# GLA's state products half way between its other steps, fewer stored split operands, own slots for raw tiles

## The chip, the cores and the metric

The kernel runs on one core of a Trainium2 chip. The metric is the time of one execution in device microseconds; the kernel before takes 1884.07 us (median of three runs, 1876.56 to 1886.29).

## The reference, cut to what matters

One inference step of a hybrid decoder layer on 2048 prompt tokens and 8 x 8 sample tokens, all in float32. Two branches run side by side on the same input, are gated and added, projected and normalised:

```python
z = jnp.einsum('btd,dn->btn', x, w_in)                       # all input projections
o_att = swa_prompt(q, k, v, attn_sink, rel_table)            # window of 128, 8 heads, 2 KV heads
def step(S, xs):                                             # GLA, per head, chunk after chunk
    qt, kt = qc * jnp.exp(b), kc * jnp.exp(-b)
    kend = kc * jnp.exp(b_last[:, None] - b)
    A = jnp.where(causal, jnp.einsum('bthk,bshk->bhts', qt, kt), 0.0)
    o = jnp.einsum('bthk,bhkv->bthv', qt, S) + jnp.einsum('bhts,bshv->bthv', A, vc)
    S = jnp.exp(b_last)[..., None] * S + jnp.einsum('bshk,bshv->bhkv', kend, vc)
    return S, o
o_gla = o_gla * lax.rsqrt(jnp.mean(jnp.square(o_gla), -1, keepdims=True) + EPS) * gla_norm_w
h_att = jnp.einsum('bta,ad->btd', o_att * jax.nn.silu(g_att), w_pa)
h_gla = jnp.einsum('btv,vd->btd', o_gla * jax.nn.silu(g_gla), w_pg)
merged = jax.nn.sigmoid(r_att) * h_att + jax.nn.sigmoid(r_gla) * h_gla
y = layer_norm(DN_ALPHA * x + merged @ w_o, ln_g, ln_b)
```

The outputs are y for prompt and samples, the last K and V rows, and the GLA states of the prompt and of the eight samples.

## The kernel before, in words

**Passes.** The large projections are eight passes over the 2112 tokens, in this order: AT (attention's q, k, v and gate, 5 blocks of 256 columns), G0, G1, G2 (the GLA heads' k, q, v and gate, 4 blocks each), PA (attention's output, half the depth), RA and RG (the two merge gates), PG (GLA's output). Then the last projection with the layer norm. A pass multiplies in seven products of block sums (a Strassen-Winograd scheme; the products are numbered 1 to 7 and taken in a listed order, for G0 to G2 1, 2, 6, 7, 5, 3, 4). Tokens are taken in three sections `s`, so a *unit* is (pass, product, section), 21 to a pass. A unit runs over the pass's 4 or 5 blocks; each is a *group*: one PSUM tile `pd` of 128 x 352, filled by twelve matmuls.

**Splits.** Each float32 operand is split into a high and a low part (`xh`, `xl` for tokens, `wh`, `wl` for weights): ACT casts the high part (L148), DVE subtracts to get the low one (L149), both in two halves of 128 x 704 for a token tile. A group's twelve matmuls are four times `xh wh`, `xl wh`, `xh wl` (L1192, L1193, L1194). A raw token tile `xs` is loaded by `raw_x` two or three units ahead; `prep_x` splits it one unit ahead. Raw tiles and split tiles share a ring of seven slots, `xb`. The same token operands serve AT, G0, G1 and G2, so some splits are stored to DRAM (`sp..h`, `sp..l`) and loaded as they are by later passes: AT stores those of products 5 and 3, G0 those of 1, 2, 4, 6 and 7. So G0 splits five of seven products and loads two, and G1 and G2 load all.

**Work between the groups.** TensorE's order is written out by hand. After each group a *tick* passes, and functions filed under that tick by `at(t, ...)` issue their instructions behind the group. Attention (`att_...`, from pass AT's end to the middle of G1) and GLA (`gla_...`, from there to the end of RG) are filed this way; their PSUM tiles are a ring of four, `pa`. The order of the other engines (ACT, DVE, POOL, SP) comes from a scheduler, and each executes its list in order.

**GLA's step.** A head's 2048 tokens are taken in 16 steps of 128, some 4.4 ticks apart. In a step `gla_v` transposes v and the decayed keys (L955, L956) and ACT copies them to `gv` (L957); `gla_a` makes the intra-chunk matrix (L965), which DVE masks (L967); `gla_b` multiplies the query with the old state (L987), makes the state product (L989) and the intra-chunk output (L990), updates the state on DVE (L995) and normalises: square on ACT (L974), two tiny operations on POOL (L975, L976), scaling on ACT (L977) into `ring`; `gla_c` transposes the normalised output (L1003) and DVE multiplies it by the gate, `sg` (L1005). `gla_v` and `gla_a` of step i stand at tick u + i (in steps), `gla_c` at u + i + 3, so one step's `gla_v` and `gla_a` share a tick with the `gla_c` of three steps before. Each step takes five tiles of the ring of four.

**Samples.** After a head's last step `samp_a` and two calls of `samp_b` make the sample outputs (`ops`) and the new sample states (L1046, L1052), four sample columns in each call's half.

The pools on the left side of SBUF are exchanged as the program goes on: `c0` at the start, `ca` for attention, `cg` for GLA, `cm` at the end (`mpool`).

## Time and profile before

| | |
|---|---|
| median of three runs | 1884.07 us (1876.56 to 1886.29) |
| the profiled execution | 1890.45 us, its span 1888.7 us |
| mean granted TensorE clock | 0.977 |
| passes AT, G0, G1, G2 | 250.6, 255.3, 211.6, 221.0 us |
| passes PA, RA, RG, PG | 114.7, 225.5, 223.5, 182.2 us |
| last projection | 199.6 us |
| DMA | 496.20 MB, 263 GB/s in the mean |

Busy times are of the profiled execution. PE is TensorE's matmul, PEld its weight load, DVE the vector engine, ACT the scalar engine, POOL GpSimd, SP the engine that issues DMAs. In a row of waits stands who waited, at which line, for whom, the total in us, how often, and the longest. In a row of the timeline stand start, duration, engine, line, operation, tiles, and in brackets the idle time ahead of it and what ended it.

### The profile page before, as it was taken

The page shows a single profiled execution, that of the slowest core. Times are in us where ns is not written, and L with a number is a line of the kernel's source. Part 1 is how long each engine was busy: PE and PEld are TensorE (multiplying, and loading weights), DVE is VectorE, ACT ScalarE, POOL GpSimd, SP SyncE. Part 2 cuts the span into 40 slices and gives each one's busy share as a digit, 9 for nine tenths or more (in the row PEclk, how much of TensorE's full clock was granted, in tenths as well). Part 3 has the DMA queues.
Part 4 walks back from the last instruction along what each step waited for, and adds up shares of the span by engine and source line. Part 5 has one row for each costly group of instructions (what it writes and reads, how often), then busy time and mean ns, then how long its engine had stood idle before and what let it go on. Part 6 is the DMA issues. An engine that isn't in the chain of part 4 may idle for free.

```text
span 1888.7 us, 30578 instructions
## 1 busy us (share of the span) xinstructions
PE 1776.7 (94%) x10587; PEld 1632.9 (86%) x10587; DVE 1302.7 (69%) x2613; ACT 857.7 (45%) x1886; POOL 413.1 (22%) x554
## 2 busy tenths in 40 slices
PE   7999898999999999999998998999899999999998
PEld 6899887887888999989888888998899999987886
DVE  5738746868757665567668876887688566876666
ACT  4333334545553346466574765676656432211100
POOL 2230103200102001321133232124331233441111
PEclk9999998999999999999999999999999999999999
DMA  9857998978868799888876886798887887896431
GB/s 307 302 199 243 326 322 322 336 262 299 300 208 288 268 325 343 286 300 269 291 220 209 277 272 221 238 300 262 287 263 251 262 287 266 254 308 206 156 120 53
DMA packets 291835, 496.20 MB, mean 263 GB/s; under 512 B 29229, under 2 KB 216869, under 8 KB 291664
## 3 DMA queue, kind: packets, MB, share of 16 engines
q1 hardware_dynamic: 290752, 493.40, 77.9%
q8 instruction: 83, 1.36, 0.3%
q0 software_dynamic: 832, 0.72, 0.2%
q14 instruction: 72, 0.59, 0.1%
q10 hardware_dynamic: 96, 0.13, 0.0%
HBM read 338.06 MB, written 156.97 MB: 262 GB/s over the span
## 4 chain that ended last, share of the span: by engine, by line
PE 59%; DMA 13%; DVE 11%; ACT 6%; POOL 5%; issue 4%; SPq 1%; DVEq 0%; POOLq 0%; ACTq 0%
PE pd L1192 14%; PE pd L1193 13%; PE pd L1194 13%; PE pd L1239 3%; PE pd L1238 3%; PE pd L1237 3%; DMA ws<-w_g 2%; POOL ws L183 2%; DVE xl L149 2%; DMA x<-xT 2%; DMA ws<-w_ra 1%; PE pa L658 1%; PE pa L708 1%; PE pa L692 1%; DVE wl L149 1%
## 5 line engine op out<-in xcount | busy, mean ns | idle before, releaser
L1192 PE MATMUL pd<-xh,wh 128*128 128x352 f32 x2484 | 845.7, 340 | 36.3 <-ACT xh L148 19.0
L1193 PE MATMUL pd<-xl,wh 128*128 128x352 f32 x2484 | 811.3, 327 | 12.5 <-DVE xl L149 12.2
L1194 PE MATMUL pd<-xh,wl 128*128 128x352 f32 x2484 | 809.4, 326 | 0.0
L1192 PEld LDWEIGHTS pd<-xh,wh 128*128 128x128 f32 x2484 | 476.9, 192 | 77.5 <-ACT xh L148 30.7
L1193 PEld LDWEIGHTS pd<-xl,wh 128*128 128x128 f32 x2484 | 478.5, 193 | 20.0 <-DVE xl L149 17.9
L1194 PEld LDWEIGHTS pd<-xh,wl 128*128 128x128 f32 x2484 | 476.1, 192 | 0.0
L183 POOL TENSOR_TENSOR ws<-ws 128x256 f32<-128x256 f32 (+1 forms) x256 | 207.5, 836 | 702.6 <-DMA ws<-w_g 278.1
L149 DVE TENSOR_TENSOR xl<-xs,xh 128x704 fp32r<-128x704 f32 (+1 forms) x228 | 196.6, 892 | 53.5 <-ACT xh L148 49.9
L149 DVE TENSOR_TENSOR wl<-ws,wh 128x512 fp32r<-128x512 f32 (+1 forms) x231 | 158.5, 692 | 97.6 <-ACT wh L148 91.6
L148 ACT CAST wh<-ws 128x512 fp32r<-128x512 f32 (+1 forms) x231 | 134.1, 591 | 191.3 <-POOL ws L183 104.7
L148 ACT CAST xh<-xs 128x704 fp32r<-128x704 f32 (+1 forms) x228 | 155.6, 723 | 79.3 <-PE pd L1193 58.5
L975 POOL TENSOR_SCALAR sq<-sq 128x1 f32<-128x1 f32 (+1 forms) x68 | 25.9, 381 | 424.1 <-ACT ring L974 423.9
L1238 PE MATMUL pd<-woh,x 128*128 128x512 f32 x256 | 102.0, 398 | 0.9 <-DVE x L149 0.9
L1237 PE MATMUL pd<-woh,x 128*128 128x512 f32 x256 | 101.3, 396 | 0.4 <-ACT woh L148 0.2
L1239 PE MATMUL pd<-wol,x 128*128 128x512 f32 x256 | 101.2, 395 | 0.6 <-DVE wol L149 0.6
L148 ACT CAST x<-xst 128x384 fp32r<-128x384 f32 (+2 forms) x48 | 22.3, 486 | 137.1 <-PE pd L1238 107.9
L672 ACT ACTIVATE s<-s,nm 128x256 f32<-128x256 f32 (+1 forms) x128 | 62.4, 489 | 42.7 <-DVE nm L669 42.7
L977 ACT ACTIVATE ring<-pa,sq 128x256 f32<-128x256 f32 (+1 forms) x68 | 32.2, 473 | 94.6 <-POOL sq L976 94.6
L259 ACT COPY a<-pd 128x352 f32<-128x352 f32 x99 | 43.7, 451 | 53.5 <-PE pd L1194 53.1
L262 DVE TENSOR_TENSOR fin<-a,pd 128x352 f32<-128x352 f32 x99 | 50.3, 513 | 23.3 <-PE pd L1194 20.9
L287 DVE TENSOR_TENSOR a<-a,pd 128x352 f32<-128x352 f32 x93 | 47.5, 514 | 23.9 <-PE pd L1194 23.5
L283 DVE TENSOR_TENSOR fin<-a,pd 128x352 f32<-128x352 f32 x93 | 47.8, 514 | 22.1 <-PE pd L1194 21.4
(250 smaller groups left out, 2548.4 us busy)
## 6 DMA issues: line engine op xcount, KB each, us to landing
xs<-xc_d SPq DMA_DIRECT2D x45, 704.0 KB
ws<-w_g SPq DMA_DIRECT2D x108, 256.0 KB
xs<-xT SPq DMA_DIRECT2D x27, 704.0 KB
xc<-tt_d SPq DMA_DIRECT2D x48, 352.0 KB
ws<-w_at SPq DMA_DIRECT2D x45, 256.0 KB
ws<-w_ra SPq DMA_DIRECT2D x36, 256.0 KB
ws<-w_rg SPq DMA_DIRECT2D x36, 256.0 KB
ws<-w_pg SPq DMA_DIRECT2D x36, 256.0 KB
```

Source lines behind the costliest of these rows:

```text
L148: pin["a"] = nc.scalar.copy(dst_h, src)
L149: i = eng.tensor_tensor(dst_l, src, dst_h.bitcast(F32), ALU.subtract)
L183: nc.gpsimd.tensor_tensor(o[:, c], x[:, c], y[:, c], op)
L262: add(z, acc[p, s, 12], ps, ALU.add)
L283: add(z, u, ps, ALU.add)
L672: nc.scalar.activation(sl, sl, AF.Exp, bias=nm[:, h:h + 1], accum_out=sm[:, h:h + 1])
L1192: mm(ps, wh[:, ks], xh[:, ts], start=(k == 0), stop=False)
L1193: mm(ps, wh[:, ks], xl[:, ts], start=False, stop=False)
L1194: mm(ps, wl[:, ks], xh[:, ts], start=False, stop=(k == q.kh - 1))
L1237: mm(ps, xh[:, xs], hi, start=(k == 0), stop=False)
L1238: mm(ps, xl[:, xs], hi, start=False, stop=False)
L1239: mm(ps, xh[:, xs], lo, start=False, stop=(k == KT - 1))
```

## The change

Four edits:

- `gla_b` of step i is filed 3/2 steps after `gla_v` of step i, not 5/4. The two calls of `samp_b` are filed one tick later.
- The sample outputs are normalised inside the first `samp_b`, ahead of its state products, not after the second.
- AT stores no splits; G0 stores those of products 1, 2, 6, 7 and 4 as before. So G0, G1 and G2 load the raw tiles of products 5 and 3 and split them themselves.
- While the pool `ca` is open, raw tiles have two slots of their own in it (`xs`); `xb` then holds only split tiles.

```diff
     def mpool(name):
         mid.close()
+        M["name"] = name
         M["p"] = mid.enter_context(tc.tile_pool(name=name, bufs=1, side="left", reuse_waits="tile"))
...
-            x = mtile("xb", F32, "xs")[:, :n]
+            if M["name"] == "ca":
+                x = mt("xs", 4 * T, 2)[:, :n]
+            else:
+                x = mtile("xb", F32, "xs")[:, :n]
...
         def stores(self, i):
-            return i in ((5, 3) if self is passes[P_AT] else (1, 2, 4, 6, 7) if self is passes[P_G0] else ())
+            return self is passes[P_G0] and i in (1, 2, 6, 7, 4)
...
                     mm(B["ops"][32 * q:32 * q + 32, :HV], B["qz"][:, 4 * q + b, :], B["S0", 4 * q][:, b, :],
                        start=False, stop=(b == 3), tile_position=(0, 32 * q))
+            gla_norm(B, "s", B["ops"][:NS, :HV], NS)
         sp = [pa(), pa()]
...
-        if j0:
-            gla_norm(B, "s", B["ops"][:NS, :HV], NS)
...
-                at(tt(u + i + 5 / 4), lambda B=B, i=i: gla_b(B, i))
+                at(tt(u + i + 3 / 2), lambda B=B, i=i: gla_b(B, i))
...
-                at(o + 5, lambda B=B: samp_b(B, 0))
-                at(o + 7, lambda B=B: samp_b(B, 2))
+                at(o + 6, lambda B=B: samp_b(B, 0))
+                at(o + 8, lambda B=B: samp_b(B, 2))
```

In the changed program the lines are numbered a little higher (L1195 for L1192, L149 for L148, L993 for L989). Three places of the order follow; numbers behind a name tell buffers apart.

TensorE at one GLA step in pass G2, from `gla_c` to `gla_b`'s third product, before:

```order
L1003 MATMUL pa_8302<-ident_197,ring_7201 128x128 x2
L955 MATMUL pa_8306<-ident_197,zvv_8010 128x128 x2
L956 MATMUL pa_8306<-ident_197,ek_8086 128x128
L965 MATMUL pa_8311<-dm_8084,em_8085 128x128
L1192 MATMUL pd_8333<-xh_7907,wh_8018 128x352
...
L987 MATMUL pa_8350<-ring_7201,gb_7836 128x256
L989 MATMUL pa_8352<-gv_7203 128x256
L990 MATMUL pa_8350<-gv_7203,aper2_211 128x256
```

and now:

```order
L1007 MATMUL pa_8326<-ident_197,ring_7209 128x128 x2
L959 MATMUL pa_8330<-ident_197,zvv_8034 128x128 x2
L960 MATMUL pa_8330<-ident_197,ek_8099 128x128
L969 MATMUL pa_8335<-dm_8097,em_8098 128x128
L1195 MATMUL pd_8357<-xh_7931,wh_8042 128x352
...
L1195 MATMUL pd_8374<-xh_7931,wh_8169 128x352
...
L991 MATMUL pa_8394<-ring_7209,gb_7849 128x256
L993 MATMUL pa_8396<-gv_7211 128x256
L994 MATMUL pa_8394<-gv_7211,aper2_211 128x256
```

`gla_b` stood one group (a `pd` tile's twelve matmuls) behind the other three, and now stands two behind; the others keep their places.

ACT in pass G0, units (1,0) and (1,1); `xh_2806` and, in the changed program, `xh_2782` are the high part for unit (1,1), whose first group is `pd_2907` and now `pd_2883`. Before:

```order
L259 COPY a12_2857<-pd_2844 128x352
L259 COPY a12_2872<-pd_2859 128x352
L259 COPY a12_2887<-pd_2874 128x352
L148 CAST xh_2806<-xs_2598 128x704 x2
L259 COPY a12_2920<-pd_2907 128x352
L148 CAST wh_2903<-ws_2804 128x512
```

and now:

```order
L149 CAST xh_2782<-xs_2578 128x704 x2
L149 CAST wh_2796<-ws_2677 128x512
L149 CAST wh_2879<-ws_2780 128x512
L149 CAST wh_2967<-ws_2867 128x512
L311 ACTIVATE th_2752<-a12_834 128x352
L149 CAST xh_2869<-xs_2673 128x704 x2
L311 ACTIVATE th_2774<-a5_859 128x352
L263 COPY a12_2813<-pd_2800 128x352
L263 COPY a12_2833<-pd_2820 128x352
L263 COPY a12_2848<-pd_2835 128x352
L263 COPY a12_2863<-pd_2850 128x352
L263 COPY a12_2896<-pd_2883 128x352
```

The cast stood behind the copies of the four groups of unit (1,0); now it and the one for unit (1,2), `xh_2869`, stand ahead of all of them.

DVE in pass G2 at the end of unit (3,1), where the operand of unit (3,2) was loaded split before; `pd_9962` is the last group of (3,1), `pd_10007` the first of (3,2), `xl_9872` the low part that (3,2) needs. Now:

```order
L291 TENSOR_TENSOR a12_8121<-a12_8121,pd_9943 128x352
L291 TENSOR_TENSOR a12_8147<-a12_8147,pd_9962 128x352
L1009 TENSOR_TENSOR sg_9715<-pa_9981,sg_9715 128x2x64
L150 TENSOR_TENSOR xl_9872<-xs_9580,xh_9871 128x704 x2
L997 COPY ring_7209<-pa_9986 128x256
L314 SCALAR_TENSOR_TENSOR a12_8147<-th_9976,a12_8147 128x352
L291 TENSOR_TENSOR a12_8186<-a12_8186,pd_10007 128x352
```

The subtract stands behind the eviction of the unit before, with no group between that and its use.

## The prediction

> **What bounds the kernel now.** I read the page first, then the busy time by pass, then the waits of TensorE in the passes that the change touches, then single waits in the timeline.

> ```profile
> span 1888.7 us, 30578 instructions
> PE 1776.7 (94%) x10587; PEld 1632.9 (86%) x10587; DVE 1302.7 (69%) x2613; ACT 857.7 (45%) x1886; POOL 413.1 (22%) x554
> ```

> TensorE is busy for 94% of the span, so an edit off TensorE can win only what TensorE now waits: 1888.7 - 1776.7 = 112 us, and the time that it runs below full clock. By pass (us, then busy time of PE, PEld, DVE, ACT, POOL with counts, granted clock, DMA share, GB/s; the rows are G0, G2, RA and RG):

> ```profile
> 255.30:510.60 255.30, 234.46 (x1417) 207.17 (x1417) 180.23 (x337) 122.12 (x329) 35.65 (x44) 0.95 0.86 304
> 722.20:943.20 221.00, 210.97 (x1296) 201.60 (x1295) 137.46 (x335) 128.41 (x275) 48.58 (x84) 0.98 0.86 291
> 1057.90:1283.40 225.50, 214.65 (x1315) 202.60 (x1314) 180.67 (x398) 146.35 (x299) 59.68 (x83) 0.98 0.81 260
> 1283.40:1506.90 223.50, 210.31 (x1264) 198.73 (x1263) 160.07 (x329) 128.52 (x265) 72.05 (x96) 0.97 0.81 264
> ```

> G0 idles 255.3 - 234.5 = 20.8 us and loses 0.05 x 255.3 = 12.8 us to the clock. G2, RA and RG idle 10.0 + 10.9 + 13.2 = 34.1 us and lose 0.02 x 221 + 0.02 x 225.5 + 0.03 x 223.5 = 15.6 us. The waits of TensorE (total, times, longest), first in G0, then from 722 to 1507 us:

> ```profile
> PE pd L1192 <- ACT xh L148: 8.5, 6, 3.3
> PE pd L1193 <- DVE xl L149: 6.9, 8, 1.9
> ...
> PE pa L989 <- DVE sg L1005: 16.1, 10, 4.3
> PE pa L989 <- ACT gv L957: 7.0, 3, 2.6
> PE pa L1046 <- ACT ring L977: 4.2, 2, 3.6
> PE pa L989 <- ACT ak L957: 3.2, 3, 2.2
> ```

> So G0 waits 15.4 us for the split of its moving operand, and the three GLA passes wait 26.3 us at one instruction, the state product L989, which needs the PSUM slot that `gla_c` (sg) or `gla_v` (gv, ak) has just used.

> One such wait, and the clock behind it (rows of 1 us):

> ```profile
> 757.91 0.59 PE L987 MATMUL pa<-ring,gb 128*128 128x256 f32 x2
> 760.88 0.83 PE L989 MATMUL pa<-gv 128*128 128x256 f32 x2 [2.38 <-DVE sg L1005]
> 762.65 0.49 PE L1193 MATMUL pd<-xl,wh 128*128 128x352 f32 x1
> 764.89 0.32 PE L1192 MATMUL pd<-xh,wh 128*128 128x352 f32 x1
> 766.80 0.32 PE L1192 MATMUL pd<-xh,wh 128*128 128x352 f32 x1
> ...
> 761.00:762.00 1.00, 1.00 (x5) 0.80 (x5) 1.00 (x4) 0.39 (x1) 0.00 (x0) 0.66 0.53 203
> 762.00:763.00 1.00, 1.00 (x5) 0.91 (x4) 0.88 (x2) 0.40 (x2) 0.00 (x0) 0.50 0.01 2
> 763.00:764.00 1.00, 1.00 (x5) 1.00 (x4) 0.00 (x0) 0.07 (x1) 0.76 (x3) 0.50 0.00 0
> 764.00:765.00 1.00, 1.00 (x6) 1.00 (x5) 0.00 (x0) 0.47 (x1) 1.00 (x3) 0.64 0.06 16
> ```

> A wait of 2.4 us is followed by a granted clock of 0.66, 0.50, 0.50, 0.64: another 0.34 + 0.50 + 0.50 + 0.36 = 1.7 us. The two L1192 rows are twelve matmuls apart, so one group of `pd` takes 1.91 us.

> [...]

> **G0, own slots for raw tiles.** With seven `xb` slots, three raw tiles, the pair in use and the next pair fill the ring, and the split stands at the very end of the unit before. ACT's casts for unit (1,1), and TensorE at that unit's start:

> ```profile
> 264.05 0.45 ACT L259 COPY a<-pd 128x352 f32<-128x352 f32 x1 [1.47 <-PE pd L1194]
> 264.40 1.46 ACT L148 CAST xh<-xs 128x704 fp32r<-128x704 f32 x2
> ...
> 265.23 0.43 PE L1192 MATMUL pd<-xh,wh 128*128 128x352 f32 x1 [1.22 <-ACT xh L148]
> 266.16 0.49 PE L1193 MATMUL pd<-xl,wh 128*128 128x352 f32 x1 [0.50 <-DVE xl L149]
> ```

> The cast is queued behind the copy of that unit's last group, so an exposed split costs 1.22 + 0.50 = 1.72 us. In the changed order ACT casts two tiles ahead, and on DVE nearly every subtract of G0 stands four to nine evictions or more ahead of its first matmul, where from the third unit of product 2 on it was none to four; only the pass's last unit stays one ahead. That such a lead is enough RA and RG show, where all 42 units are split in place one unit ahead:

> ```profile
> L1192 PE MATMUL pd<-xh,wh 128*128 128x352 f32 x672 | 231.0, 344 | 0.3 <-DVE fin L262 0.3
> L1193 PE MATMUL pd<-xl,wh 128*128 128x352 f32 x672 | 217.9, 324 | 0.0
> ```

> So the 15.4 us go, and of the clock the same share, 15.4 / 20.8 of 12.8 = 9.5. Together -24.9. Bounds: -33.6 (all of G0's idle and clock) and 0. I stay near the first, since the RA and RG rows are the same work.

> **Fewer stores.** Gone are 2 x 3 x 2 = 12 stores and 3 x 12 = 36 loads of 704 KB; 18 raw loads of 704 KB come instead: 30 x 0.72 = 21.6 MB less. TensorE waits for hardly any load in these passes, so this is 0 by itself; were G0 held by its 304 GB/s, its own twelve loads less six would give 4.3 MB or -14 us. Added are 18 units x 2 halves of cast and subtract:

> ```profile
> L149 DVE TENSOR_TENSOR xl<-xs,xh 128x704 fp32r<-128x704 f32 (+1 forms) x228 | 196.6, 892 | 53.5 <-ACT xh L148 49.9
> L148 ACT CAST xh<-xs 128x704 fp32r<-128x704 f32 (+1 forms) x228 | 155.6, 723 | 79.3 <-PE pd L1193 58.5
> ```

> 36 x 0.892 = 32 us of DVE and 36 x 0.723 = 26 us of ACT over three passes, under TensorE's work. G0's DVE goes to 180.2 + 12 x 0.892 = 191 us in some 230, 83%; RA has 80% (180.67 of 225.5) and L1192 waits 0.3 us there. For attention's chains, which get shorter units, I add +2 (bounds 0 and +7, a doubling of the 5.4 us that G0 idles outside the splits, and one clock loss). Without the cover each unit costs 1.72 + 1.7. In the changed order four splits stand late: G0 (4,2) and G2 (3,1) one eviction ahead, where a group of 1.91 us covers most, 0.9 each; G1 (3,2) and G2 (3,2) none ahead, 1.72 and half a clock loss, 2.6 each. Together +7 (0 to 14).

> In AT the units (5,1) and (3,1) no longer wait, since the subtracts move from 0 to 2 ahead to five ahead:

> ```profile
> PE pd L1193 <- DVE xl L149: 2.0, 2, 1.0
> ```

> That is -2.0 (0 to -2).

> **State products half way.** `gla_b` issues two or three products on TensorE, one update on DVE, square and scaling on ACT, two tiny operations on POOL, and no DMA. It moves past one group of twelve matmuls, 64 times: 1.91 us later. Waits up to that go: of 26.3 us there stay 4.3 - 1.9 = 2.4, 2.6 - 1.9 = 0.7 and about 1 for the others between 1.9 and 2.4, so 4. What is late next is `gla_a`, whose slot the DVE update L995 releases. Four updates ended less than 1.9 us ahead of it, the first and last of them:

> ```profile
> 913.01 0.47 DVE L995 SCALAR_TENSOR_TENSOR ring<-ring,e,pa 128x256 f32<-128x256 f32 x1
> 914.16 0.39 PE L965 MATMUL pa<-dm,em 128*128 128x128 f32 x2
> ...
> 1115.58 0.47 DVE L995 SCALAR_TENSOR_TENSOR ring<-ring,e,pa 128x256 f32<-128x256 f32 x1
> 1117.54 0.39 PE L965 MATMUL pa<-dm,em 128*128 128x128 f32 x2
> ```

> Slacks of 0.7 and 1.5 become waits of 1.2 and 0.4, and four of about 0.85 make +3.4; groups queue behind `gla_a`. Clock: L989's share, 26.3 / 34.1 of 15.6 = 12, less a quarter for the waits left, so -9. Together -26.3 + 4 + 3.4 - 9 = -28 (bounds -38 and 0). The scaling on ACT waits up to 4.9 us for POOL, which eats none of this: its reader `gla_c` comes a step and a half (six groups, 12 us) later.

> **Sample outputs.** The norm goes ahead of `samp_b`'s state products, and both steps shift with `gla_b`, so L1046's 4.2 us stay as they are: 0 (-8 with its clock, +4).

> **Sum.** -24.9 + 2 + 7 - 2 - 28 = -46. The profiled execution took 1890.45 us, 1.75 around its span; it would be 1844. It lies 6.4 above the median 1884.07, so the median becomes 1838.

> **Rivals.** *Two slots are too few.* A third raw load waits in SP's queue until the first is split; the `fin` stores and weight loads stand behind it, then evictions. For: DMA is 86% busy in G0. Against: the loads are issued two units ahead. Half of G0's gain goes and the four late splits double: 1838 + 12 + 7 = 1857. *The norm becomes the wait.* L987 takes the slot that ACT's scaling L977 frees, and sq waits on POOL. For: L1046 already waits 3.6 us so. Against: from one `gla_b` to the next the distance is unchanged. If 10 of 28 us remain won: 1856. *Slower:* the newly split units of G0, G1 and G2 are all exposed, as most split units of G0 are now, because ACT and DVE reach the split only behind the last eviction. 18 x (1.72 + 1.7) = +62; with G0's present waits kept as well, 1884 - 28 - 2 + 62 = 1916. It decides from 9 units on (9 x 3.4 = 30). Against it: the changed order has two of them with no lead, and one with one. *More:* G0 runs without any wait (-33.6) and L1046's wait goes with its clock (-8): 1884 - 46 - 9 - 8 = 1821. *The step moves but not its wait,* since DVE and ACT are reordered with it, and the splits wait for loads: about 1880. Against: `gla_c` and `gla_v` keep their places on TensorE.

> **How the numbers follow.** Forecast 0.56; too few slots 0.16; norm 0.10; more 0.07; no effect 0.05; slower 0.06. The likeliest is 1838. Its own bounds of the unknown costs, about 18 either way, with the two rivals behind it, give 1816 to 1868; "slower", "no effect" and a part of the rest lie outside. A difference under 0.5% (9.4 us) can't be told from none here. Faster by more: 0.56 + 0.16 + 0.10 + 0.07 less 0.03 of mishaps summed = 0.86; the same 0.08, slower 0.06.

> **What would show it.** Right: G0 under 235 us, with L1192 and L1193 waiting under 3 us there and a clock of 0.98 or more; L989's waits from 26 to under 8 us; one or two new waits on xl at the last units of pass G1 and G2; DMA written and read 21.6 MB lower; DVE about 32 us busier. Wrong: L1192 waiting for xs loads or evictions in G0; L965 or L987 waiting over 10 us for DVE's update or for ACT ring L977; new waits on xh and xl through G2's products 5 and 3.

## The result, and the profile after

The changed kernel takes 1859.63 us in the median of four runs (1854.89 to 1866.12), the kernel before 1883.82 us beside it: a ratio of 0.988, 95% interval 0.983 to 0.993. So it is faster, by 24 us where 46 were forecast. The profiled execution after took 1854.89 us, the shortest of its runs, and that of before 1890.45, longer than all its timed runs; the two profiles differ by 35.6 us, of which about 11 lie in AT, PG and the tail, where the change has only some 2 to win. The six passes from G0 to RG, which hold most of what the change touches, sum to -24.0 us, close to the difference of the medians, 24.2.

The head of the page of the changed kernel, and its busy time by pass (G0, G1, G2, then PA, RA and RG together; columns as before):

```profile
span 1853.1 us, 30656 instructions
PE 1759.0 (95%) x10587; PEld 1621.3 (87%) x10587; DVE 1322.2 (71%) x2649; ACT 879.4 (47%) x1922; POOL 416.5 (22%) x554
```

```profile
248.20:486.80 238.60, 225.50 (x1418) 200.83 (x1418) 178.84 (x343) 126.35 (x334) 26.68 (x35) 0.98 0.82 284
486.80:702.50 215.70, 210.69 (x1426) 193.28 (x1426) 154.00 (x326) 110.16 (x272) 18.10 (x24) 0.99 0.79 271
702.50:915.10 212.60, 207.84 (x1290) 200.01 (x1289) 137.38 (x325) 124.70 (x267) 50.56 (x84) 0.98 0.79 263
```

```profile
915.10:1475.80 560.70, 527.78 (x3205) 501.31 (x3204) 427.88 (x944) 348.55 (x745) 164.89 (x232) 0.98 0.80 258
```

G0 went from 255.3 to 238.6 us (forecast 22 less), G1 from 211.6 to 215.7, G2 from 221.0 to 212.6, and PA to RG only from 563.7 to 560.7. DVE and ACT have 36 instructions more each, as forecast, but only 19.5 and 21.7 us for the forecast 32 and 26; the DMAs moved 474.56 MB for 496.20, the forecast 21.6 less. What TensorE waits for, first in G0, then from G2 to RG (the lines are 3 to 5 later than before: L1195 and L1196 for L1192 and L1193, L712 and L696 for L708 and L692, L993 for L989, L969 for L965, L1051 for L1046):

```profile
PE pa L712 <- DVE s L665: 6.8, 1, 6.8
PE pa L696 <- DVE s L686: 3.3, 2, 2.5
PE pd L1195 <- DVE es L677: 1.5, 1, 1.5
PE pd L1196 <- DVE xl L150: 1.3, 1, 1.3
```

```profile
PE pa L993 <- DVE sg L1009: 8.1, 5, 2.5
PE pa L969 <- DVE ring L999: 4.7, 6, 1.9
PE pd L1196 <- DVE xl L150: 4.6, 1, 4.6
...
PE pa L1051 <- ACT ring L981: 4.3, 2, 2.3
...
PE pa L969 <- DVE sg L1009: 1.6, 1, 1.6
PE pa L959 <- DVE ring L999: 1.0, 1, 1.0
```

In G0 the waits for the split went from 15.4 to 1.3 us, and attention's waits came up from 5.3 to 11.6. In the GLA passes the state product's waits went from 26.3 to 8.3 us (8.1 and a 0.2 that this view leaves out), the instructions behind the state update wait 7.3 us that they did not wait before (4.7 + 1.6 + 1.0), and one late split in G2 takes 4.6 us.

**How runs are compared below.** One program's times spread by over 1%: 29 runs of the kernel before, beside the first experiments, go from 1866 to 1892 us. Most of that is the clock. Every run has its span and its mean granted clock, and span x (1 - clock) is what the clock lost: 24 to 45 us in those 29 runs, 39.5 in the median. The time without that loss is steadier, 1838.6 to 1852.1 us in those runs, so the table has both. Ratios are of medians against the kernel before on the same chip.

| kernel | median us | ratio (95%) | clock's loss | time less the loss |
|---|---|---|---|---|
| before (29 runs) | 1880.8 | 1 | 39.5 | 1843.6 |
| the change | 1859.6 | 0.988 (0.983-0.993) | 31.6 | 1827.8 |
| E1 half step alone | 1874.7 | 0.996 (0.994-0.999) | 33.7 | 1841.4 |
| E3 own slots alone | 1873.4 | 0.997 (0.994-1.000) | 36.5 | 1837.6 |
| E4 fewer stores alone | 1867.5 | 0.993 (0.990-0.995) | 36.4 | 1827.9 |
| E2 slots and stores | 1857.3 | 0.988 (0.984-0.992) | 30.6 | 1827.1 |
| E14 G0 splits all itself | 1865.1 | 0.991 (0.988-0.995) | 35.4 | 1831.8 |
| E13 stores, copies added | 1853.4 | 0.983 (0.980-0.987) | 28.7 | 1824.5 |
| E15 before, weights first | 1898.3 | 1.008 (1.005-1.011) | 41.8 | 1855.6 |

### The profile page after: what moved, and what is told of

The parts are those of the page before. It is cut to its first block, busy times and chain, and to the rows that moved or that the text cites. A ratio compares the mean times of both kernels' runs of the same rounds, so it can differ in the third digit from the quotient of the medians.

```text
span 1853.1 us, 30656 instructions
## 1 busy us (share of the span) xinstructions
PE 1759.0 (95%) x10587; PEld 1621.3 (87%) x10587; DVE 1322.2 (71%) x2649; ACT 879.4 (47%) x1922; POOL 416.5 (22%) x554
## 2 busy tenths in 40 slices
DMA packets 290970, 474.56 MB, mean 256 GB/s; under 512 B 28749, under 2 KB 220997, under 8 KB 290800
## 5 line engine op out<-in xcount | busy, mean ns | idle before, releaser
L1195 PE MATMUL pd<-xh,wh 128*128 128x352 f32 x2484 | 837.9, 337 | 30.0 <-ACT xh L149 10.8
L1196 PE MATMUL pd<-xl,wh 128*128 128x352 f32 x2484 | 805.4, 324 | 10.1 <-DVE xl L150 9.6
L1195 PEld LDWEIGHTS pd<-xh,wh 128*128 128x128 f32 x2484 | 472.3, 190 | 68.8 <-issue 32.0
L1196 PEld LDWEIGHTS pd<-xl,wh 128*128 128x128 f32 x2484 | 473.9, 191 | 15.3 <-DVE xl L150 13.7
L150 DVE TENSOR_TENSOR xl<-xs,xh 128x704 fp32r<-128x704 f32 (+1 forms) x264 | 232.6, 906 | 66.4 <-ACT xh L149 56.1
L149 ACT CAST xh<-xs 128x704 fp32r<-128x704 f32 (+1 forms) x264 | 182.8, 731 | 102.5 <-PE pd L1196 64.9
L149 ACT CAST wh<-ws 128x512 fp32r<-128x512 f32 (+1 forms) x231 | 134.2, 591 | 184.8 <-POOL ws L184 90.2
L979 POOL TENSOR_SCALAR sq<-sq 128x1 f32<-128x1 f32 (+1 forms) x68 | 21.7, 319 | 437.3 <-ACT ring L978 437.3
L149 ACT CAST x<-xst 128x384 fp32r<-128x384 f32 (+2 forms) x48 | 22.3, 486 | 137.5 <-PE pd L1241 107.3
L1278 DVE SCALAR_TENSOR_TENSOR z<-xr,pd 128x512 f32<-128x512 f32 (+1 forms) x36 | 23.6, 656 | 56.0 <-PE pd L1242 55.7
L1241 PEld LDWEIGHTS pd<-woh,x 128*128 128x128 f32 x256 | 48.0, 187 | 15.3 <-DVE x L150 4.0
```

Of the source, the lines that this page charges most:

```text
L149: pin["a"] = nc.scalar.copy(dst_h, src)
L150: i = eng.tensor_tensor(dst_l, src, dst_h.bitcast(F32), ALU.subtract)
L1195: mm(ps, wh[:, ks], xh[:, ts], start=(k == 0), stop=False)
L1196: mm(ps, wh[:, ks], xl[:, ts], start=False, stop=False)
L1241: mm(ps, xl[:, xs], hi, start=False, stop=False)
```

## The experiments

**E1, the half step alone.** The kernel before with only this (the two sample steps one group later as well):

```diff
-                at(tt(u + i + 5 / 4), lambda B=B, i=i: gla_b(B, i))
+                at(tt(u + i + 3 / 2), lambda B=B, i=i: gla_b(B, i))
```

> The kernel before with edit 1 alone: gla_b 3/2 steps after gla_v instead of 5/4, samp_b one tick later. Theory A (the prediction's mechanism with its size: the waits at the state product go, up to one group of 1.91 us each): -28 us, L989's waits from 26 to under 8 us. Theory B (the waits follow the step, since the norm of gla_b holds ACT back, ACT holds the splits on DVE back, and sg stands behind these): about -10 us, half of L989's waits left or turned into waits at L965. G0 unchanged under both.

It gave 1874.67 us, ratio 0.9962 (0.9935 to 0.9990): -7 us, where the prediction's theory (A) had -28 and theory B, that the wait follows the step, -10. The busy time of G2 and of PA to RG with the step alone, and of PA to RG in the kernel before:

```profile
716.90:930.30 213.40, 209.68 (x1291) 201.15 (x1290) 129.15 (x321) 122.24 (x262) 50.01 (x86) 0.98 0.88 298
930.30:1494.10 563.80, 527.23 (x3205) 500.50 (x3204) 432.41 (x946) 349.38 (x748) 167.79 (x232) 0.98 0.79 256
```

```profile
943.20:1506.90 563.70, 528.32 (x3199) 499.93 (x3198) 428.21 (x937) 346.89 (x737) 164.28 (x232) 0.98 0.80 255
```

In the passes that the step reaches, all of the gain is in G2, 221.0 to 213.4 (the two profiles also differ where the step does nothing). From PA to RG, where 42 of the 60 state updates are, 563.7 stays 563.8. The waits of TensorE from G2 to RG in this run:

```profile
PE pa L989 <- DVE sg L1005: 10.1, 6, 3.1
PE pa L965 <- DVE ring L995: 8.1, 8, 2.3
PE pa L1046 <- ACT ring L977: 6.5, 3, 2.9
...
PE pa L955 <- DVE ring L995: 2.1, 2, 1.8
```

L989 gave back 14 us of its 26.3 (1.8 at ak are left beside the 10.1). Of these 8.1 + 2.1 came back at the next users of the slot that the update L995 frees, and 2.3 at the sample products.

**E3, E4, E2: the other two edits, apart and together.** E3 is the kernel before with own raw slots, E4 with the new rule for stores, E2 with both.

```diff
...
+            if M["name"] == "ca":
+                x = mt("xs", 4 * T, 2)[:, :n]
...
-            return i in ((5, 3) if self is passes[P_AT] else (1, 2, 4, 6, 7) if self is passes[P_G0] else ())
+            return self is passes[P_G0] and i in (1, 2, 6, 7, 4)
```

> Own slots alone; AT stores products 5 and 3 as before, so G1 and G2 load all splits. If the gain of G0 comes from the slots, G0 shortens by 15 to 20 us and the run by 15 to 20 us, more than e2 (no late splits in G1 and G2). If it comes from the missing stores, under 5 us.

> Fewer stores alone; raw tiles stay in the ring of seven. By the prediction this edit alone costs: the splits of G0 stay late (its waits of 15 us stay, products 5 and 3 join them) and the late splits of G1 and G2 come on top: 0 to +10 us. If the 21.6 MB of transfers were what bounds G0 to G2, it gains 15 us or more.

> The kernel before with edits 3 and 4 (fewer stores, own slots), the GLA step as before. Theory A (prediction): -18 us (G0 -24, new late splits +7). Theory C (two slots of their own are too few: SP waits for a split before it can issue the raw load, ACT waits for that load, attention's steps stand behind): -10 to -14 us, with G0 near 239 us and two or three waits of TensorE on attention's DVE work (3 to 7 us each).

E3 1873.40 us (-7), E4 1867.49 (-13), E2 1857.33 (-23, ratio 0.9881, 0.9839 to 0.9922). E2 is as fast as the whole change: the half step and the earlier sample norm add nothing to it that these runs can tell (1859.6, and 1827.8 without the clock's loss where E2 has 1827.1). And the edit that the prediction priced at a loss, fewer stores, brings most of it. The forecast for E3 (15 to 20 us, or under 5) met neither of its two cases. TensorE's waits in G0, with own slots alone and with fewer stores alone:

```profile
PE pa L712 <- DVE s L665: 9.5, 1, 9.5
PE pa L696 <- DVE s L686: 5.7, 1, 5.7
PE pd L1197 <- DVE xl L150: 3.0, 3, 1.5
```

```profile
PE pd L1192 <- ACT xh L148: 5.9, 3, 3.2
PE pa L708 <- DVE s L661: 3.7, 1, 3.7
PE pd L1193 <- DVE xl L149: 3.4, 4, 1.3
```

Own slots take 12.4 of the 15.4 us off the split, as forecast, and attention takes 10.6 back: 5.3 became 15.9 (with 0.7 that is not shown). Fewer stores take off only 6.1, but attention gives 1.6 as well. G0 is 244.9 with the one, 241.7 with the other, 239.8 with both. With fewer stores alone G1 is 7.3 us longer than before (218.9), with its late splits, and G2 7.3 shorter (213.7).

**E14 and E13: why fewer stores gain.** E14 lets G0 store all seven products and AT none: G0 then splits 5 and 3 itself, while G1 and G2 load every pair as before. E13 is E4 with the saved traffic and issues given back, as copies that nothing reads; of its diff the copies alone are shown.

```diff
-            return i in ((5, 3) if self is passes[P_AT] else (1, 2, 4, 6, 7) if self is passes[P_G0] else ())
+            return self is passes[P_G0]
```

```diff
             x = mtile("xb", F32, "xs")[:, :n]
+            if i in (5, 3) and self in (passes[P_G0], passes[P_G1], passes[P_G2]):
+                for _ in range(2):
+                    nc.sync.dma_start(du_d[next(du)], io["x"][:P, :640])
...
```

> The kernel before, but AT stores nothing and G0 stores all seven products: G0 splits 5 and 3 itself and loads no pair, G1 and G2 load all 21 pairs each as before. Theory G: G0 gains as with fewer stores alone (255 to about 242, without its clock loss 243 to 233), but G1 and G2 stay at 211 and 221 with SP's 41 us of waits at the pair loads in G2; the ratio 0.992 to 0.995. If G2's gain is only the place of the GLA steps against the units: G2 at 214 too.

> Fewer stores alone, plus two copies from DRAM to DRAM, 128 x 640 floats (0.33 MB) each, issued by SP at each of the 18 raw loads of products 5 and 3 in G0, G1 and G2; nothing reads them. They give back the 21 to 24 MB of traffic that fewer stores took away and 36 of its 30 to 48 issues on SP. Theory F (fewer stores gain by the traffic or by SP's issues): back to 1875 to 1882, against 1867.5 for fewer stores alone, and G2 back to 218 or more from 213.6. Theory G (they gain because a loaded pair claims two of the seven slots from the moment of its issue, so its load stands in SP's queue until TensorE has read the old pair, with the weight loads behind it): within 4 us of 1867.5.

E14: 1865.09 us, ratio 0.9913 (0.9876 to 0.9949). Its G0 and G2:

```profile
251.70:490.50 238.80, 228.73 (x1419) 204.38 (x1417) 181.99 (x343) 127.07 (x336) 27.57 (x34) 0.96 0.87 308
...
703.60:921.70 218.10, 209.37 (x1296) 199.89 (x1295) 134.68 (x331) 126.05 (x270) 48.84 (x84) 0.99 0.87 294
```

G0 alone makes the gain, at 308 GB/s, and G2 keeps 218 of its 221 us. E13 moved 307 GB/s in G0 where E4 moved 277:

```profile
243.10:478.80 235.70, 226.28 (x1418) 201.25 (x1418) 180.10 (x343) 126.97 (x337) 25.32 (x32) 0.99 0.87 307
```

Each copy is read and written, and with both counted all of the saved traffic is back, 497.0 MB (E4 has 473.4). The kernel before, then E13:

```profile
HBM read 338.06 MB, written 156.97 MB: 262 GB/s over the span
```

```profile
HBM read 336.88 MB, written 160.11 MB: 268 GB/s over the span
```

It was not slower but faster, 1853.44 us, which neither theory had. So neither the traffic nor SP's issues are what fewer stores save, and the prediction's 0 for transfers stands. What is left is the reading of theory G: a loaded pair claims two of the seven slots from its issue on, a raw tile one, so without pairs in G0 the splits come further ahead: by the traces 12 of the 15 units that G0 split before had their split done less than 2 us ahead of the unit's first matmul, or later than it; in E4 it is 7 of 21, and 1 of 21 in the change. That the claim is the cause is argued from these leads and from E14, not shown by an edit of its own. Why E13 beats E4 by 14 us (in the medians 8 by the clock, 3.5 without it) stays open; the copies also change SP's order, which no run tells apart.

**E15 and E16: weights first.** In SP's program the weight loads of the next unit come ahead of the operand loads, in the kernel before (E15) and in the change (E16).

```diff
+        issue_w(n + 1)
         issue_x(n + 2)
         if n:
             issue_x(n + 3)
-        issue_w(n + 1)
```

> The kernel before, with the weight loads of the next unit issued on SP ahead of the operand loads of the units after it, and nothing else. Theory G (weights come late because they stand behind pair loads that wait for a slot; ACT, DVE and TensorE are then late in turn): the waits for late weights go, G0 and G2 lose 5 us or more together, ratio 0.990 to 0.996. If weights are not what is late: ratio 0.998 to 1.004, since operand loads have two units of slack.

> The whole change with the weight loads issued ahead of the operand loads. In G0 of the change the weights of a unit land 5 to 6 us after GpSimd is ready for them, ACT's cast, DVE's subtract and attention's score evictions stand behind (TensorE waits 6.8 us at L712). If that chain is the cause of attention's waits: G0 at 230 to 234 where the change has 238.6, time 1848 to 1855. If it is attention's own chain or the raw loads: within 3 us of 1859.6.

E15 was slower, 1898.32 us, ratio 1.0081 (1.0051 to 1.0110): L1192's wait in G0 rose from 8.5 to 13.1 us, and G0 from 255.3 to 261.7. E16 gave 1862.56, no difference, with 6.3 us at L712. So in G0 of the kernel before the operand loads have no slack in SP's queue. That late weights are what costs there, half of theory G, is not borne out.

**E5, E17, E18: what attention now waits for.** The one long wait of G0 after the change. Rows of ACT, then DVE, then TensorE around it:

```profile
315.20 0.62 ACT L149 CAST wh<-ws 128x512 fp32r<-128x512 f32 x1 [4.18 <-POOL ws L184]
319.12 1.46 ACT L149 CAST xh<-xs 128x704 fp32r<-128x704 f32 x2 [3.29 <-DMA xs<-xc_d]
```

```profile
319.93 2.22 DVE L150 TENSOR_TENSOR xl<-xs,xh 128x704 fp32r<-128x704 f32 x2 [2.95 <-ACT xh L149]
...
323.41 0.69 DVE L150 TENSOR_TENSOR wl<-ws,wh 128x512 fp32r<-128x512 f32 x1 [0.83 <-ACT wh L149]
324.02 2.47 DVE L665 SCALAR_TENSOR_TENSOR s<-pa,bias 128x512 f32<-128x512 f32 x4
```

```profile
324.85 1.97 PE L712 MATMUL pa<-pT,vt 128*64 128x512 f32 x4 [6.79 <-DVE s L665]
```

ACT stands for the weights and then for the raw operand, DVE's subtracts stand for ACT, and the score evictions L665 stand behind both on DVE although their inputs are there. E5 cuts the two own slots into five halves, each freed as soon as it is split (a raw tile is loaded in two transfers). E17 gives product 7's second raw weight tile a slot of its own, E18 both of its tiles three slots, with three half slots for the operand.

Of the diffs of E5 and E17, the lines that set the slots:

```diff
+                    x = tuple(mt("xs", 2 * T, 5) for _ in range(2))
...
```

```diff
-                t = self.wtile("ws", p)
+                t = self.wtile("ws", p) if M.get("name") != "ca" or i != 7 or not out else mt("w7", 512, 1)[:, :self.kh * P]
```

> The whole change, but in the attention stage the two own slots for raw tiles become five slots of half a tile each; a raw tile is loaded in two transfers, and a half is free again as soon as it is split. Theory C (two own slots are too few: the third raw load stands in SP's queue until a split has freed a slot, ACT's cast then stands waiting for that load, and attention's score evictions on DVE stand behind the subtract): the waits of TensorE in G0 at L712 and L696 (6.8 and 3.3 us, with 5.1 us of clock) fall by half or more, SP's wait at the raw load falls from 23 us to under 10, the time to 1850 to 1855, against 1859.6 for the change. Theory A (the prediction: two slots suffice, what attention waits is its own chain): within 3 us of 1859.6.

> The whole change, with one more slot in the attention stage, for the second raw weight tile of product 7. Theory H: the rest of attention's waits in G0 comes from product 7's weights. Product 6's sums and differences hold eight of the ten ws slots until products 5 and 3, so the pairs of raw tiles for product 7 come through two slots: load, GpSimd's difference, ACT's cast, DVE's subtract, next load, some 7 us a turn (pairs of loads issued at 308.7, 315.2 and 322.8 us), and on DVE the score evictions stand behind that subtract. A third slot lets a load go out before the difference is done: TensorE's wait at L712 falls from 6.8 us to under 4, with its 3.4 us of clock G0 goes from 238.6 to 230 to 235, time 1850 to 1856. If the scores are late for another reason: L712 still 6 us or more, time within 3 us of 1859.6.

> The whole change, with both raw weight tiles of product 7 in three slots of their own in the attention stage (five with the two free ws slots' room unused), paid for by cutting the two own raw operand slots to three half tiles. Theory H: as with one slot, since three in place of two; L712 under 4 us, G0 at 230 to 235, and if three half tiles are too few for the operands, waits at L1195 and L1196 in G0 grow from 1.3 to 5 us or more. If weights are not the cause: L712 at 6 us or more.

1859.67, 1861.83 and 1857.75 us: no difference from the change. In E5 SP's wait at the raw loads fell from 23.0 to 16.7 us only. The wait stays, 6.3, 5.8 and 7.2 us; here E18:

```profile
PE pa L714 <- DVE s L667: 7.2, 1, 7.2
...
```

In E17 ACT's cast waited less for the weight (1.80 us for 4.18) and more for the raw operand (5.20 for 3.29). Two inputs are late there, one behind the other, and mending one leaves the other; no run mended both, so the cause is open further back.

**E6: the late splits.** G0 stores all seven products in the changed kernel, so G1 and G2 split nothing.

> The whole change, but G0 stores the split operands of all seven products, so G1 and G2 load every one of them again and split nothing: 12 stores and 24 loads more, 12 raw loads less, 704 KB each. Theory D (the three late units of G1 and G2 cost 13 us with their clock, as the trace of the change has it): G1 211 and G2 205 to 208 us where the change has 215.7 and 212.6, G0 within 3 us of 238.6, the time 1846 to 1850. The prediction's size for the same three units: 6 us, so 1853. If the additional 25 MB bound these passes: 1870 or more.

1857.85 us, no difference. G1 is 211.0 as forecast there, but G2 213.1 where theory D had 205 to 208. The first wait from G1 to G2 in its list:

```profile
PE pa L1051 <- ACT ring L981: 2.7, 1, 2.7
```

It ends 163.2 us into G2, where the change's late split ended 161.0 us into it, and the clock lost 3.4 us behind each. The late split of 4.6 us lay over a wait that comes up when it goes.

**E8: a fifth slot for the waiting products.** The eight PSUM slots of the two pools cut five to three instead of four to four.

```diff
-    psd = ctx.enter_context(tc.tile_pool(name="psd", bufs=4, space=PSUM))
-    psa = ctx.enter_context(tc.tile_pool(name="psa", bufs=4, space=PSUM))
+    psd = ctx.enter_context(tc.tile_pool(name="psd", bufs=3, space=PSUM))
+    psa = ctx.enter_context(tc.tile_pool(name="psa", bufs=5, space=PSUM))
```

> The whole change with the eight PSUM banks cut otherwise: five for pa (attention, GLA, samples) and three for pd (the main products), where it is four and four. If the waits in G0 and the GLA passes are waits for a slot of pa that comes free late, as the prediction reads them (L993, L969, L712, L696: 26 us in all after the change, with 12 or so of clock), they fall by two thirds and the time to 1835 to 1845, less what pd's evictions then cost in PA (10 us of waits now, up to 20). If they are waits for DVE's and ACT's own lateness, which hits pd just as much: no gain, 1860 to 1875.

1860.59 us, no difference. TensorE's waits from G2 to RG now begin with

```profile
PE pd L1195 <- DVE a L269: 9.2, 5, 3.7
PE pd L1195 <- ACT a L263: 8.2, 5, 3.4
PE pd L1195 <- DVE fin L266: 7.5, 8, 2.1
```

L993 is gone from the head of the list and the main product waits instead. From G2 to RG TensorE idles 40.6 us in E8 (busy for 737.3 of 777.9), 37.7 in the change and 45.4 before. So one more slot for the waiting products won nothing. The main product has one slot less here, so this run alone can't tell engines that are late anyway from the price of that slot; E1 and E2, with the rows below, decide on the half step.

**What makes them late** shows at 1333.9 us in the change. DVE:

```profile
1329.16 0.69 DVE L150 TENSOR_TENSOR wl<-ws,wh 128x512 fp32r<-128x512 f32 x1 [3.11 <-ACT wh L149]
1329.77 0.51 DVE L266 TENSOR_TENSOR fin<-a,pd 128x352 f32<-128x352 f32 x1
1331.38 0.89 DVE L150 TENSOR_TENSOR xl<-xs,xh 128x704 fp32r<-128x704 f32 x1 [1.09 <-ACT xh L149]
1332.19 0.51 DVE L269 TENSOR_TENSOR a<-a,pd 128x352 f32<-128x352 f32 x1
1332.62 0.88 DVE L150 TENSOR_TENSOR xl<-xs,xh 128x704 fp32r<-128x704 f32 x1
1333.42 0.42 DVE L1009 TENSOR_TENSOR sg<-pa,sg 128x256 f32<-128x256 f32 x1
```

DVE stood idle for 3.1 and 1.1 us for ACT's casts with sg queued behind them; the transposes that sg reads had ended at 1326.5. ACT itself had waited 1.95 us for GpSimd's weight difference. All five waits at L993 for sg in the change are of this kind: sg began 5.4 to 8.5 us after its input was ready, and DVE stood idle for 2.1 to 5.3 us of that, four times for ACT and once for a DMA. Of the ten in the kernel before, seven have 0.6 to 2.0 us of such idle time; in the other three DVE was busy with what stands ahead of sg in its list.

**E7: is it GpSimd in the norm?** Its two small operations per `gla_norm` left out.

```diff
-        nc.gpsimd.tensor_scalar(sq[:n], sq[:n], EPS, None, op0=ALU.add)
-        nc.gpsimd.tensor_tensor(sq[:n], sq[:n], mhalf[:n], ALU.pow)
```

> The whole change without the two small GpSimd operations of every gla_norm: the output is scaled by the mean square itself and not by its inverse root, so this part of the computation is left out; the square, the scaling and their places on ACT stay. Theory B (the state products wait because ACT holds the scaling until GpSimd has done sq, so that the casts, DVE's subtracts and sg behind them come late): the waits in G2, RA and RG at L993, L969 and L1051 (8.1, 6.3 and 4.3 us in the trace of the change) fall by half, with clock -8 to -14: 1846 to 1852. Theory A (the reader of the scaled output comes six groups later, so it costs nothing): within 3 us of 1859.6.

1841.53 us, ratio 0.9807 (0.9769 to 0.9846): 18 us less than the change, 11 without the clock's loss. But not where theory B had it. From G2 to RG:

```profile
PE pa L969 <- DVE ring L997: 8.6, 8, 2.3
PE pa L991 <- DVE sg L1007: 7.4, 4, 4.0
...
PE pa L969 <- DVE sg L1007: 2.4, 1, 2.4
```

These lines wait 18.4 us, where the change has 14.4 (8.1 + 4.7 + 1.6). The samples' product L1051 went from 4.3 to 1.3, and PA from 116.3 to 109.0 us: there the main product's waits for DVE's and ACT's evictions fell from 11.6 to 5.7. So the two GpSimd operations cost the change some 11 to 18 us, and they aren't what holds the state products. ACT stands for them for 91.4 us (94.6 before); how much of the cost is that standing and how much is GpSimd's own work, this run can't tell.

**E9 to E12: the scaling later.** ACT's scaling issued one group (E9, E11, E12) or two (E10) behind the square; E11 on the kernel before, E12 on the change with the old place of the step.

```diff
-        nc.scalar.mul(on[:n], o, sq[:n])
+        at(now[0] + 1, lambda: nc.scalar.mul(on[:n], o, sq[:n]))
```

> The whole change, and ACT's scaling in gla_norm is issued one group of the main product later than the square, so that GpSimd's sq is done when ACT comes to it; nothing is left out. Theory B (ACT stands at the scaling for GpSimd, 91 us in 62 waits between the middle of G2 and the end, and casts, subtracts and sg stand behind it): ACT's wait for sq falls to under 40 us, PA loses 4 us or more, the time is 1843 to 1851 against 1859.6, most of what leaving GpSimd's two operations out gave. If the PSUM slot held one group longer is what counts: waits at L969, L993 and L1051 for ACT's scaling of 10 us or more, 1860 to 1870.

> The same with two groups. Theory B: ACT's wait for sq falls to almost nothing, but the slot of pa is held 3.8 us longer, and the next use of it is about two groups behind, so new waits for ACT's scaling appear at TensorE: within 5 us of the one-group version, on either side. If ACT's wait alone counted: 3 to 5 us faster than the one-group version.

> The kernel before with only ACT's scaling one group later; the state products stay where they were. Theory B (the 26 us at L989 are there because ACT, and DVE behind it, are late, so they go when ACT is freed and not when the products are moved): L989's waits fall by half or more, with clock -10 to -18, ratio 0.990 to 0.995. Theory A (it is the place of the state products that makes the wait): no change, ratio 0.998 to 1.002.

> The whole change without its step (state products and sample steps back at their old places), with ACT's scaling one group later. It tells whether the half step is worth something once ACT is free: by the prediction's sizes the step is worth 20 us or more, so 1865 or more here; by theory B the step moved the wait only from L993 to L969, so within 4 us of the one-group version of the whole change.

1859.32, 1862.54, 1878.98 (ratio 0.998, 0.9958 to 1.0002) and 1861.82 us. The edit did not do what it was for: the scaling stands directly behind the square 45 times of 68 in E9 as in the change, and ACT's wait in E9 is what it was (91.4 us):

```profile
ACT ring L981 <- POOL sq L980: 91.5, 57, 6.3
```

So E9 to E11 say nothing on theory B. E12 is of use for another thing: it is the change without its half step, and within 3 us of it and of E9.

## Why the prediction was right or wrong

Right in direction, and inside its range, but the gain is half of the forecast. By its steps, in the two profiles:

| step | forecast | measured |
|---|---|---|
| G0: waits for the split | -15.4 | -14.1 |
| G0: clock | -9.5 | -6.8 |
| attention's chains | +2 (0 to +7) | +6.3 |
| late splits in G1 and G2 | +6 | G1's pass +4.1; G2's nothing by E6 |
| AT's two units | -2.0 | -2.3 at L1193 |
| GLA step: L989's own waits | -22.3 | -18.0 |
| GLA step: new waits behind the update | +3.4 | +7.3 |
| GLA step: clock | -9 | -1.7 |
| GLA step in all | -28 | -7 alone, nothing on top of the rest |

**The step that failed is "State products half way", -28.** Its arithmetic took each wait as a fixed delay of one slot, from which 1.91 us could be taken by coming 1.91 us later, with the update following 1.91 us later and the rest at no cost. Alone it brought -7 us, and on top of the other edits nothing that the runs can tell. The waits at L989 did shrink nearly as forecast. But most of them were the place where TensorE met a DVE and an ACT that were late by themselves, DVE idle for ACT's cast with sg behind it. E1 has the same time from PA to RG, 563.8 for 563.7, with 10 us of waits moved to L965 and L955. The updates did not follow by 1.91 us either: of the four whose slack the prediction read at L995, only one became a wait in E1, of 0.2 us. The other seven waits of L965 there stand at steps whose updates had 2.7 to 6.3 us of slack before, and they last up to 2.3 us.

**The clock was mis-sized twice**, as a share of the waited time. Waits of 0.25 to 1.5 us that stood apart lost nothing (last section), while one of 3.60 us, L1046 at 1291.8 us before, lost 3.4 and one of 4.25 us, L989 at 1150.0, lost 1.7; so -9 for the GLA step came to -1.7. By these numbers a wait cut in two can save the whole loss, and one moved whole need not save any.

**Own slots:** the mechanism was right, and so was its size for the split. What was missed is the other side. Once the split no longer stops TensorE, it reaches attention earlier, and the score evictions stand on DVE behind the same casts; +2 was taken and +6.3 came, near the upper bound, and +10.6 with own slots alone.

**Fewer stores:** priced at nothing to +7, measured -13 alone, -16 without the clock's loss. The text looked at the transfers, where E13 agrees that there is nothing, and at the added splits. It left out that the pairs that G0 no longer loads claim slots of the ring whose shortage it had just described for the edit beside it; that this is the cause fits the leads and E14, which puts the gain in G0, but is argued. So G0's gain came by two cures for what looks like one wait, and they do not add up: G0 lost 10.4 us with own slots alone, 13.6 with fewer stores alone and 15.5 with both, and the whole time without the clock's loss 6, 16 and 16.5 (the medians, with that loss in them, 7, 13 and 23). That the time came to lie inside the range is luck: what fewer stores gained made up for most of what the half step did not bring.

**G2's gain was counted as the step's.** E1 takes G2 to 213.4, E4 without the step to 213.7, both together to 212.6: one saving, which either edit gives. How fewer stores gives it is not shown; E14, which loads all pairs in G2, does not have it (218.1).

**Sample outputs:** 0 was forecast, and L1051 waits 4.3 us for 4.2. **Rivals:** "two slots are too few" had 1857 and "the norm becomes the wait" 1856, both nearer to the time than the forecast, but neither by its cause. The forecast without its clock terms (-9.5, -9 and the 1.7 us in the late splits) would be about 1855, nearer too, but G0 alone lost 6.8 us less to the clock. Finer slots gained nothing (E5), though SP waited 23.0 us at the raw loads; and ACT waited for sq 94.6 us before and 91.4 after, so the norm did not become the wait.

**What stays open:** what makes the raw operand and the weights late together near 312 us in G0; why ACT's casts are late in the GLA passes, which was followed back for one wait only; why E13 is 14 us faster than E4; and why leaving out GpSimd's small operations saves time in PA when the waits that it was to mend stay. No version here is surely faster than the change: E13's interval overlaps it, and E7 leaves work out.

## What to carry to other kernels

Before a wait for a buffer is booked as a gain, ask whether its releaser is late by itself: look when the releaser's input was ready, and what its engine stood for until it ran. If that engine was late anyway, moving the waiting instruction moves the wait. In a ring of buffers, count what each kind of load claims from its issue on; the gains of two edits that relieve the same ring must not be summed before a run has both. Price the clock by the idle time that falls into one of its windows (3413 ns in these traces, below), not as a share of all waiting.

## What the hardware showed that was not expected

```profile
1297.68 0.70 PE L993 MATMUL pa<-gv 128*128 128x256 f32 x2 [2.46 <-DVE sg L1009]
```

```profile
1298.00:1299.00 1.00, 1.00 (x7) 0.92 (x6) 0.93 (x3) 1.00 (x3) 1.00 (x1) 1.00 1.04 328
```

```profile
1333.89 1.22 PE L993 MATMUL pa<-gv 128*128 128x256 f32 x2 [2.54 <-DVE sg L1009]
```

```profile
1334.00:1335.00 1.00, 1.00 (x3) 0.82 (x4) 0.04 (x1) 0.50 (x2) 0.00 (x0) 0.50 1.01 376
```

One cost nothing and the other 1.71 us. The clock records in the 20 profiles of this case show what sets them apart. In the profiles before and after, the recorded clock is 1.00 or 0.50, and each stretch at 0.50 lasts 3413 or 6827 ns, but for the last, in which the recording ends (6399 and 6410 ns). In each of the 20, all changes of the granted clock (598 together, 41 of them before and 25 after) lie a whole number of windows of 3413 ns apart, to within 5 ns. Cut each execution into these windows and sum what TensorE idles in each. After 9959 windows at full clock with less than 1.3 us of idle time the clock never fell; after all 200 with 2.0 us or more the next window ran at half clock, which loses 1.7 us; of 270 in between, 89 were followed by one. In the profiles before and after alone these are 0 of 994, all 21, and 13 of 31. The first of the two waits was cut by a border and left 1.91 us in one window, the second 1.95.

So where a wait falls counts as well as how long it is. Of 98 waits of 1.75 to 2.5 us with no other within 7 us, 44 cost nothing, 48 cost 1.7 us and 6 cost 3.4; of 331 of 0.25 to 1.5 us none cost clock; of 14 above 5 us, 11 were followed by 3.4 us of loss and three by 5.1, part of it still within the wait. The windows begin at another place in each of the 20 executions, 0.1 to 3.1 us after the first instruction. That fits the spread of one program's times, though no run here fixes that place.
